# Matmul operands of a two-layer hybrid network moved to addresses that are multiples of 256 bytes

## The chip, the cores and the metric

The kernel runs on one core of one Trainium2 chip. The metric is device time in microseconds (us) of one execution; the median of three executions of the kernel before is 2283.09 us (2277.65 to 2285.34).

## The reference

Two layers over 512 tokens of 1024 channels. Each layer is a feed-forward block, a token mixer, and a second feed-forward block, each on an RMS norm of its input and added back; a last norm ends it. Layer 0 mixes with RWKV-7 and block attention, layer 1 with HGRN2. All of it is float32.

```python
def swiglu(h, w_gate, w_up, w_down):
    return (jax.nn.silu(h @ w_gate) * (h @ w_up)) @ w_down
...
    for l in range(DEPTH):
        x = x + 0.5 * swiglu(rmsnorm(x, norm_g[l, 0]), ffn1_wg[l], ffn1_wu[l], ffn1_wd[l])
        h = rmsnorm(x, norm_g[l, 1])
        if l % 2 == 0:
            p = h @ ev_w_in[e]
            y_a = rwkv7_mix(p[..., :RWKV_COLS], ...)
            y_b = moba_mix(p[..., RWKV_COLS:], slopes)
            y = jnp.concatenate([y_a, y_b], axis=-1) @ ev_w_out[e]
        else:
            y = hgrn2_mix(h @ od_w_in[o], lb_table[l], hg_norm_w[o]) @ od_w_out[o]
        x = x + y
        x = x + 0.5 * swiglu(rmsnorm(x, norm_g[l, 2]), ffn2_wg[l], ffn2_wu[l], ffn2_wd[l])
    return rmsnorm(x, final_g)
```

## The kernel before

**Tiling.** Channels lie on the 128 partitions, tokens along the free dimension. The 512 tokens are two streams of 256: stream 0 (A) and stream 1 (B). Both go through the same stages, one after the other or interleaved, so each stream has half of every kind of product.

**Three products for one.** A float32 product is made of three matmuls in the type float32r (`mm3`). The weights are split into a high plane `wh` and a low plane `wl`, the activations into `hh` and `hl` (input of a stage; `hh0`, `hl0` of stream 0 and `hh1`, `hl1` of stream 1) or `ah` and `al` (the inner activation of a feed-forward block). `mm3` multiplies high by high, low by high and high by low into one PSUM bank of the pool `pmm` (tile `m`). The weight block, 128 x 128, is the loaded operand; the activation plane, 128 x 256, is the one that streams through ("moving"). In `rows` (values of the mixers) it is the other way round: 512 columns of a weight plane stream, and a block of `hh` or `hl` is loaded.

**Jobs.** `run` goes through a list of jobs, one for each 128 x 1024 (or 128 x 768) piece of weights: a DMA from SyncE into `wr` (3 places), a copy of it into `wh` on ScalarE, the rest into `wl` on VectorE (3 places each), then the matmuls of the piece. Pieces are split two jobs ahead. A feed-forward block (`ffn`) has jobs `gate` and `up` (moving `hh`, `hl`) and `down` (moving `ah`, `al`). The mixers run as tasks whose steps `fill` puts between the matmuls by a rough model of the engines (`Clock`), which sees operations and tiles, not addresses. Their products go into tiles `b`, mostly as float32 matmuls, which the trace shows as two records each.

**Addresses.** Tiles come from pools (`K.__init__`: `cp` constants, `wp` weights, `hp` activations), and a pool lays its tags out in the order in which each is first asked for, in steps of 32 bytes. The allocation of the kernel before gives these places on every partition:

| planes | bytes from | multiple of 256 plus |
|---|---|---|
| `x0`, `x1` | 16512, 24704 | 128 |
| `wr`, `wh`, `wl` (all places) | 39232, 51520, 63808 | 64 |
| `hh0`, `hl0` | 76096, 84288 | 64 |
| `hh1`, `hl1` | 117632, 125824 | 128 |
| `ah`, `al` (all places) | 102144, 109312 | 0 |
| `acc`, `tmp` | 92480, 94528 | 64 |
| `tu`, `bc0` | 100096, 99072 | 0 |

The last column is called the residue below. Within a plane every moving operand begins at a multiple of 1024 bytes and every loaded block at a multiple of 512 bytes, so all operands of a plane have the plane's residue.

Of the kernel before, what the change touches and what calls it, by code (L numbers as in the profile page):

```python
# [22 lines left out]
# blocks of d_ff whose sums meet in PSUM, and the parts that a load takes  # L23
# [12 lines left out]
LEAD = -0.2  # L36

# [43 lines left out]
class Clock:  # L81
    """A rough model of when the engines get to their work; it only orders the program."""
# [8 lines left out]
    def tile(self, name, key, bufs):  # L91
        """a tile takes a free place, or the one that is done with first"""
        ring = self.slots.setdefault(key, [])
        rec = {"base": 0.0, "end": 0.0, "acc": []}
        if len(ring) < bufs:
            ring.append(rec)
        else:
            i = min(range(bufs), key=lambda x: ring[x]["end"])
            rec["base"] = rec["end"] = ring[i]["end"]
            ring[i] = rec  # L100
        self.recs[name] = rec
# [84 lines left out]
class Stream:  # L186
    """one half of the tokens"""


class K:  # L190
    def __init__(self, tc, ctx, a):
        self.tc, self.a = tc, a
        nc = self.nc = tc.nc
        self.clk = Clock()
        self.pe = Eng(nc.tensor, "pe", self.clk)
        self.v = Eng(nc.vector, "dve", self.clk)
        self.s = Eng(nc.scalar, "act", self.clk)
        self.g = Eng(nc.gpsimd, "pool", self.clk)
        self.q = Eng(nc.sync, "dma", self.clk)
        self.mm = self.pe.matmul  # L200
        self.n = 0
        self.tasks, self.named, self.marks = [], {}, {}
        self.pending, self.micro = [], []
        self.ticks, self.left = 0, 0.0
        self.cp = ctx.enter_context(tc.tile_pool(name="const", bufs=1))
        self.wp = ctx.enter_context(tc.tile_pool(name="wts", bufs=1))
        self.hp = ctx.enter_context(tc.tile_pool(name="act", bufs=1))
        self.ppm = ctx.enter_context(tc.tile_pool(name="pmm", bufs=3, space=PSUM))
        self.ppx = ctx.enter_context(tc.tile_pool(name="pmx", bufs=5, space=PSUM))
        self.st = []  # L210
        for i in range(2):
            st = Stream()
            st.i = i
            st.x = self.t(self.cp, [128, KT, N], F32, f"x{i}", 1)
            st.acc = None
            st.hready = 0.0
            self.st.append(st)
        self.par = self.t(self.cp, [128, NPAR], F32, "par", 1)
        self.cst = self.t(self.cp, [128, NCST], F32, "cst", 1)
        self.msk = self.t(self.cp, [128, NMSK], U8, "msk", 1)  # L220
        self.q.dma_start(self.st[0].x[:, 0:2], a["x"][0][:, 0:2])
        self.q.dma_start(self.par, a["par"])
        warm = self.t(self.cp, [128, 1], F32, "warm", 1)
        self.g.memset(warm, 0.0)
        self.s.activation(warm, warm, AF.Tanh)
        self.ident, self.id64, self.blk = self.c("ident"), self.c("id64"), self.c("blk")
        self.gmask, self.sel, self.ones = self.c("gmask"), self.c("sel"), self.c("ones")

    def loads(self):
        """what the first products do not wait for"""  # L230
        nc, a = self.nc, self.a
        self.q.dma_start(self.st[1].x, a["x"][1])
        n = CST["dist"][0]
        self.q.dma_start(self.cst[:, n:], a["cst"][:, n:])
# [8 lines left out]
    def t(self, pool, shape, dtype, tag, bufs):  # L243
        self.n += 1
        x = pool.tile(shape, dtype, tag=tag, name=f"{tag}_{self.n}", bufs=bufs)
        self.clk.tile(x.name, (id(pool), tag), bufs)
        return x

# [21 lines left out]
    # ---- order of the program: a list of jobs on the weights, and tasks that fill in  # L270
# [26 lines left out]
    def fill(self, until=0.0):  # L297
        """a step of a task that its engine need not wait for; more of them while PE waits anyway"""
        free = self.clk.free
        while True:  # L300
            now = max(free["pe"], until)
            full = max(free["dve"], free["act"]) > now + self.left + BACK
            for t in self.eligible():
                if t.ready <= max(now, free[t.eng]) + LEAD and (t.first or not full):
                    self.step(t)
                    break
            else:
                return
            if free["pe"] >= until:
                return  # L310
# [8 lines left out]
    def due(self, all):  # L319
        """the evacuations of the last jobs whose time has come"""  # L320
        now = [z for z in self.pending if all or not z[1]]
        self.pending = [(ev, hold - 1, name) for ev, hold, name in self.pending if hold and not all]
        for ev, _, name in now:
            if name:
                self.need(name)
            yield ev()
# [7 lines left out]
    def spread_out(self, done):  # L334
        """what goes along with a job, at its place in the job"""
        while self.micro and self.micro[0][0] <= done:
            self.micro.pop(0)[1]()
# [83 lines left out]
    # ---- pieces  # L421
# [4 lines left out]
    def mm3(self, out, w, x, first, last):  # L426
        """out += w^T x with w = (hi, lo) and x = (hi, lo)"""
        self.mm(out, w[0], x[0], start=first, stop=False)
        self.mm(out, w[0], x[1], start=False, stop=False)
        self.mm(out, w[1], x[0], start=False, stop=last)  # L430
        self.left -= out.free_size() / 800
        self.spread_out(1.0 - self.left / self.total)
        self.ticks += 1
        if self.ticks % TICK == 0:
            self.fill()
# [14 lines left out]
    # ---- rms norm of the columns of x^T: x * g goes into the products, and what they give is scaled  # L450
    def squares(self, st, i, last=False):
        """adds the squares of the pair i of row tiles; where PE has nothing else to do, it adds the rest"""
# [18 lines left out]
    def scaled(self, st, gi, i):  # L471
        """the pair i of row tiles of x^T * g, in two parts"""
# [10 lines left out]
    def inv_rms(self, st):  # L483
        """1 / rms, by token on the partitions"""
# [10 lines left out]
    def spread(self, st):  # L495
        """1 / rms on all partitions"""
# [25 lines left out]
    def norm(self, st, n):  # L522
        """starts the task of the norm n: (name, row of norm_g, whether it is done before the products)"""
# [29 lines left out]
    # ---- feed-forward  # L553
    def ffn(self, st, l, which, norm, then):
# [32 lines left out]
        def down(i, f0, f1, g0, g1):  # L587
            """the blocks f0 to f1 of the group g0 to g1"""
            def go(w):
# [4 lines left out]
                for d in range(2):  # L594
                    for j in range(m):
                        # the first product clears the marks of the bank, so that it opens both sums
# [31 lines left out]
        for f0, f1 in GRP:  # L628
            # one block past the group
# [12 lines left out]
    # ---- y^T (hi, lo) through the output projection, added to x^T  # L642
# [32 lines left out]
    def rows(self, st, srcs, evac):  # L675
        """h @ w for 512 columns, tokens on the partitions"""
# [24 lines left out]
    # ---- layer 0  # L701
# [22 lines left out]
    def proj0(self, st):  # L724
        """the jobs by part; the first of them waits for the scale"""
# [10 lines left out]
        def go(b, i):  # L736
            """the block b of columns, the first (i = 0) or the second of a pair that shares a bank"""
# [55 lines left out]
    # ---- MoBA: two blocks of 256 and one past block at most, so that a query sees all tokens up to it  # L793
    def moba(self, st):
        pool, v, s, mm, half = self.pool, self.v, self.s, self.mm, st.i
        for qi in range(2):
# [4 lines left out]
            for pr in range(4):  # L801
# [6 lines left out]
                for e, (sb, pe, sm) in enumerate(es):  # L808
                    # minus the scores, and minus their maximum
# [27 lines left out]
    # ---- RWKV-7: [channel of a pair of heads, pair, token]; chunks of 64 tokens  # L837
# [74 lines left out]
    def bcast(self, bc, rn):  # L912
        """[token, pair and head] -> [channel of a pair, pair, token]"""
# [70 lines left out]
    def rw_inv(self, env, c):  # L984
        """(I - A)^-1, the blocks on the diagonal doubled"""
# [56 lines left out]
    def rw_tail(self, st, q, env):  # L1042
        """norm per head, bonus, gate"""
# [7 lines left out]
        # r and k of these tokens end here  # L1051
# [28 lines left out]
    # ---- layer 1: HGRN2  # L1080
    def setup1(self, pool):
# [11 lines left out]
        # (1 - lb) / 2, its negative  # L1093
# [8 lines left out]
    def proj1(self, st, norm):  # L1102
# [9 lines left out]
        def go(b):  # L1112
            def f(w):
# [8 lines left out]
                def ev():  # L1122
# [10 lines left out]
                    if b < 16:  # L1133
                        th = self.t(self.hp, [128, 2, N], F32, "tmp", 2)
                        s.activation(th, o, AF.Tanh, scale=0.5)
                        for i in range(2):
                            c = j + i
                            # f = lb + (1 - lb) sigmoid, k = (1 - lb) (1 - sigmoid)
# [38 lines left out]
    def hg_levels(self, st, q, env):  # L1177
        """scores of 128 tokens: for every level, the second half of a block against the first; the
        products of the decays from the block's middle to either side stay in [0, 1]"""
# [109 lines left out]
# norms that end before the products that read them start  # L1289
# [3 lines left out]
def _cut(jobs, n):  # L1293
    """the first n jobs, and the rest; a negative n counts from the end"""
# [5 lines left out]
def _held(jobs, name, n):  # L1300
    """the first n jobs of a stage are evacuated together, after the task of the scale"""
# [47 lines left out]
def _tiles(w):  # L1349
    """[K, C] -> [C / 128, 128 (row in tile), K]: a block of 128 columns per entry"""  # L1350
# [5 lines left out]
def _down(w):  # L1356
    """[F, D] -> [D / 256, 128, 2 * F]: for a group of row tiles, 2 blocks of columns by the tiles"""
# [4 lines left out]
def _rows(w):  # L1362
    """[D, 512] -> [4, 128, 2 * 512]"""
    return np.ascontiguousarray(w.reshape(4, 2, 128, 512).transpose(0, 2, 1, 3).reshape(4, 128, 1024))
# [47 lines left out]
```

## Time and profile before

| | |
|---|---|
| median of three runs | 2283.09 us |
| span of the profiled execution | 2278.3 us |
| TensorE matmul busy | 2246.6 us (99%), 20476 records |
| VectorE, ScalarE busy | 1640.6 us (72%), 1061.7 us (47%) |
| granted TensorE clock, mean | 0.996 |

The profiled execution's own time is known by its span; it lies 4.8 us under the median and inside the spread of the three runs. "Busy" of TensorE counts matmuls from their start to their modelled end. They are pipelined and overlap, so what one costs is read from the distance between the starts of neighbours, not from its duration.

### The profile page before, as it was taken

What the parts mean: (1) busy time and instruction counts of PE and PEld (TensorE: products, weight loads), DVE (VectorE), ACT (ScalarE), POOL (GpSimd) and SP (SyncE); (2) the same over time, 40 slices, a digit from 0 to 9 for tenths busy, and PEclk for the clock granted to TensorE, in tenths of its full rate; (3) what the DMA queues carried; (4) which work ended last, traced back from release to release, by engine and by line L of the source; (5) the groups of instructions that cost most, each with busy time, mean ns of one, the idle gap of its engine ahead of it and who ended that gap; (6) DMA issues with size and microseconds to landing.
All of it is one profiled execution on the core that took longest, in us unless ns stands there. A gap on an engine that the chain in (4) does not pass through costs nothing.

```text
span 2278.3 us, 48851 instructions
## 1 busy us (share of the span) xinstructions
PE 2246.6 (99%) x20476; PEld 2176.9 (96%) x20476; DVE 1640.6 (72%) x2863; ACT 1061.7 (47%) x1716; POOL 3.7 (0%) x15
## 2 busy tenths in 40 slices
PE   8999999999999999999999999999999999999998
PEld 8999989899999888999998999999999999999998
DVE  6867758576677666776777786677777776767776
ACT  5545544345554434544454344454455334445444
POOL 0000000000000000000000000000000000000000
PEclk9999999999999999999999999999999999999999
DMA  6565524345554233456654345665665434556664
GB/s 224 180 198 175 172 87 137 96 133 178 190 168 157 74 103 98 147 163 182 181 189 157 130 139 151 190 179 178 192 183 172 151 118 154 160 185 195 191 191 136
DMA packets 107644, 363.64 MB, mean 160 GB/s; under 512 B 12064, under 2 KB 12192, under 8 KB 107296
## 3 DMA queue, kind: packets, MB, share of 16 engines
q1 hardware_dynamic: 107424, 360.53, 50.9%
q8 instruction: 160, 2.62, 0.5%
q14 instruction: 60, 0.49, 0.1%
HBM read 358.38 MB, written 2.10 MB: 158 GB/s over the span
## 4 chain that ended last, share of the span: by engine, by line
PE 93%; DVE 4%; ACT 2%; issue 1%; DMA 1%; SPq 0%; DVEq 0%; ACTq 0%
PE m L175 81%; PE b L175 12%; DVE wl L175 2%; ACT wh L175 1%; DMA wr<-in_f1gu 1%; DVE x L175 0%; DVE tmp L175 0%; DVE hl L175 0%; ACT hh L175 0%; DVE m L175 0%; DVE acc L175 0%; ACT tmp L175 0%; DVE rqz L175 0%; SPq L175 0%; ACT sh L175 0%
## 5 line engine op out<-in xcount | busy, mean ns | idle before, releaser
L175 PE MATMUL m<-hh,wh 128*128 128x256 f32 x3808 | 1095.9, 288 | 13.1 <-ACT wh L175 10.2
L175 PE MATMUL m<-hh,wl 128*128 128x256 f32 x3808 | 1074.2, 282 | 5.7 <-DVE wl L175 5.6
L175 PE MATMUL m<-hl,wh 128*128 128x256 f32 x3808 | 1073.7, 282 | 0.4
L175 DVE TENSOR_TENSOR wl<-wr,wh 128x1024 fp32r<-128x1024 f32 (+2 forms) x725 | 832.2, 1152 | 312.7 <-ACT wh L175 304.6
L175 ACT CAST wh<-wr 128x1024 fp32r<-128x1024 f32 (+2 forms) x725 | 712.7, 989 | 540.5 <-PE m L175 387.8
L175 PEld LDWEIGHTS m<-hh,wh 128*128 128x128 f32 x3808 | 724.6, 190 | 28.2 <-ACT wh L175 11.0
L175 PEld LDWEIGHTS m<-hh,wl 128*128 128x128 f32 x3808 | 724.3, 190 | 8.3 <-DVE wl L175 8.3
L175 PEld LDWEIGHTS m<-hl,wh 128*128 128x128 f32 x3808 | 724.6, 190 | 2.5 <-DVE hl L175 1.5
L175 PE MATMUL m<-ah,wh 128*128 128x256 f32 x1408 | 400.1, 284 | 0.0
L175 PE MATMUL m<-al,wh 128*128 128x256 f32 x1408 | 391.6, 278 | 0.0
L175 PE MATMUL m<-ah,wl 128*128 128x256 f32 x1408 | 391.4, 278 | 0.0
L175 PEld LDWEIGHTS m<-ah,wh 128*128 128x128 f32 x1408 | 264.5, 188 | 7.6 <-issue 5.1
L175 PEld LDWEIGHTS m<-ah,wl 128*128 128x128 f32 x1408 | 265.9, 189 | 0.0
L175 PEld LDWEIGHTS m<-al,wh 128*128 128x128 f32 x1408 | 264.9, 188 | 1.0 <-issue 1.0
L175 ACT CAST ah<-tu 128x256 fp32r<-128x256 f32 x176 | 71.5, 406 | 308.9 <-DVE tu L175 308.8
L175 DVE SCALAR_TENSOR_TENSOR tu<-tu,m 128x256 f32<-128x256 f32 x352 | 146.9, 417 | 6.5 <-ACT tu L175 0.5
L175 DVE TENSOR_TENSOR al<-tu,ah 128x256 fp32r<-128x256 f32 x176 | 74.9, 425 | 84.3 <-ACT ah L175 84.3
L175 DVE SCALAR_TENSOR_TENSOR x<-m,x 128x512 f32<-128x512 f32 x128 | 87.9, 687 | 20.3 <-PE m L175 20.0
L175 DVE TENSOR_TENSOR m<-m,bc 128x512 f32<-128x512 f32 x118 | 81.9, 696 | 21.5 <-PE m L175 16.8
L175 ACT ACTIVATE tu<-m 128x256 f32<-128x256 f32 x176 | 66.8, 380 | 21.0 <-DVE m L175 20.3
L175 PE MATMUL b<-Rq,Rk 128*128 128x128 f32 (+2 forms) x576 | 59.5, 252 | 0.0
L175 PEld LDWEIGHTS b<-Rq,Rk 128*128 128x128 f32 (+2 forms) x576 | 55.3, 167 | 3.8
(204 smaller groups left out, 1456.4 us busy)
## 6 DMA issues: line engine op xcount, KB each, us to landing
wr<-in_f2gu SPq DMA_DIRECT2D x176, 512.0 KB, 3.7
wr<-in_f1gu SPq DMA_DIRECT2D x175, 512.0 KB, 3.6
wr<-in_f1d SPq DMA_DIRECT2D x96, 384.0 KB, 3.3
wr<-in_f2d SPq DMA_DIRECT2D x96, 384.0 KB, 3.3
wr<-in_od_in SPq DMA_DIRECT2D x48, 512.0 KB, 3.4
wr<-in_ev_in SPq DMA_DIRECT2D x44, 512.0 KB, 3.3
wr<-in_f1d SPq DMA_DIRECT2D x16, 512.0 KB, 3.7
wr<-in_ev_out SPq DMA_DIRECT2D x16, 512.0 KB, 3.4
```

Of the source, the lines that this page charges most:

```text
L175: return f(*args, **kw)
```

## The change

No operation is added, removed or reordered. Only the order in which tags are first asked for changes, and with it the addresses. The constants `par`, `cst`, `msk`, `warm` are placed first, then a tile of 192 bytes that nothing uses, then `x0` and `x1`. A new helper `places` asks once for a tile of each plane, so that the planes lie first in their pools; the small tiles (`ms2`, `rqi`, `rqz`, `r0`, `r1`, `rqy`) come behind them.

```diff
+PAD = 192
...
+        self.par = self.t(self.cp, [128, NPAR], F32, "par", 1)
+        self.cst = self.t(self.cp, [128, NCST], F32, "cst", 1)
+        self.msk = self.t(self.cp, [128, NMSK], U8, "msk", 1)
+        warm = self.t(self.cp, [128, 1], F32, "warm", 1)
+        self.t(self.cp, [128, PAD], U8, "pad", 1)
         self.st = []
         for i in range(2):
...
-        self.par = self.t(self.cp, [128, NPAR], F32, "par", 1)
-        self.cst = self.t(self.cp, [128, NCST], F32, "cst", 1)
-        self.msk = self.t(self.cp, [128, NMSK], U8, "msk", 1)
+
+        self.places(self.wp, ("wr", KT * 128, F32, 1 + LOADS), ("wh", KT * 128, F32R, AHEAD + 1),
+                    ("wl", KT * 128, F32R, AHEAD + 1))
+        self.places(self.hp, *((f"{n}{i}", KT * N, F32R, 1) for i in range(2) for n in ("hh", "hl")),
+                    ("ah", N, F32R, 7), ("al", N, F32R, 7), ("acc", 2 * N, F32, 1), ("tmp", 2 * N, F32, 2),
+                    ("tu", N, F32, 2), ("bc0", N, F32, 1), ("bc1", N, F32, 1))
         self.q.dma_start(self.st[0].x[:, 0:2], a["x"][0][:, 0:2])
         self.q.dma_start(self.par, a["par"])
-        warm = self.t(self.cp, [128, 1], F32, "warm", 1)
         self.g.memset(warm, 0.0)
...
+    def places(self, pool, *tags):
+
+        for tag, n, dtype, bufs in tags:
+            self.n += 1
+            pool.tile([128, n], dtype, tag=tag, name=f"{tag}_{self.n}", bufs=bufs)
```

## Rows read from the trace of the kernel before

**Rows 1.** The page: busy time, and TensorE, VectorE and its clock in 40 slices.

```profile
PE 2246.6 (99%) x20476; PEld 2176.9 (96%) x20476; DVE 1640.6 (72%) x2863; ACT 1061.7 (47%) x1716; POOL 3.7 (0%) x15
...
DVE  6867758576677666776777786677777776767776
...
PEclk9999999999999999999999999999999999999999
```

**Rows 2.** The page: chain that ended last, as shares of the span.

```profile
PE 93%; DVE 4%; ACT 2%; issue 1%; DMA 1%; SPq 0%; DVEq 0%; ACTq 0%
PE m L175 81%; PE b L175 12%; DVE wl L175 2%; ACT wh L175 1%; DMA wr<-in_f1gu 1%; DVE x L175 0%; DVE tmp L175 0%; DVE hl L175 0%; ACT hh L175 0%; DVE m L175 0%; DVE acc L175 0%; ACT tmp L175 0%; DVE rqz L175 0%; SPq L175 0%; ACT sh L175 0%
```

**Rows 3.** Waits: engine, what for, total us, times, longest us.

```profile
ACT wh L175 <- PE m L175: 387.8, 263, 4.5
...
PE m L175 <- ACT wh L175: 10.2, 5, 5.8
...
PE m L175 <- DVE wl L175: 5.6, 9, 0.8
```

**Rows 4.** Groups of instructions: matmuls of the planes, count, busy us, mean ns.

```profile
L175 PE MATMUL m<-hh,wh 128*128 128x256 f32 x3808 | 1095.9, 288 | 13.1 <-ACT wh L175 10.2 <-ACT hh L175 2.7 <-ACT tmp L175 0.2
...
L175 PE MATMUL m<-al,wh 128*128 128x256 f32 x1408 | 391.6, 278 | 0.0
L175 PE MATMUL m<-ah,wl 128*128 128x256 f32 x1408 | 391.4, 278 | 0.0
...
L175 PE MATMUL m<-wh,hh 128*128 128x512 f32 x96 | 39.7, 414 | 0.7 <-ACT RV L175 0.7
```

**Rows 5.** Chain, unbroken gate/up stretches, stream 0, then 1: start, us, matmuls.

```profile
105.76 34.56 PE m L175 x288
...
1416.05 33.92 PE m L175 x288
```

**Rows 6.** Chain, unbroken down stretches, streams 0, 0, 1, 1: start, us, matmuls.

```profile
140.32 16.36 PE m L175 x144
...
1047.11 16.35 PE m L175 x144
...
1449.97 16.96 PE m L175 x144
...
1993.53 16.35 PE m L175 x144
```

**Rows 7.** Four of these stretches: us, busy (records) of PE, PEld, DVE, ACT, POOL; clock.

```profile
105.84:140.27 34.43, 34.43 (x289) 34.43 (x288) 26.87 (x40) 16.58 (x24) 0.00 (x0) 1.00 0.60 183
1416.12:1449.92 33.80, 33.80 (x289) 33.80 (x288) 22.33 (x32) 15.65 (x23) 0.00 (x0) 1.00 0.60 184
1047.18:1063.41 16.23, 16.23 (x145) 16.23 (x144) 11.38 (x15) 7.80 (x10) 0.00 (x0) 1.00 0.71 198
1450.05:1466.88 16.83, 16.83 (x145) 16.83 (x144) 10.22 (x13) 6.97 (x10) 0.00 (x0) 1.00 0.71 192
```

**Rows 8.** Groups within two stretches of rows 6, 1047.11 then 1449.97: count, mean ns.

```profile
L175 PE MATMUL m<-ah,wl 128*128 128x256 f32 x47 | 13.0, 276 | 0.0
...
L175 PE MATMUL m<-ah,wl 128*128 128x256 f32 x47 | 13.2, 281 | 0.0
```

**Rows 9.** Stretch at the lower granted clock, stream 0: clock, then first and tenth start.

```profile
1206.60:1209.80 3.20, 2.78 (x13) 2.78 (x14) 2.52 (x6) 1.56 (x2) 0.00 (x0) 0.50 0.47 164
...
1207.40 0.41 PE L175 MATMUL m<-hh,wh 128*128 128x256 f32 x1
...
1209.32 0.41 PE L175 MATMUL m<-hh,wh 128*128 128x256 f32 x1
```

**Rows 10.** 512-column matmuls, stream 0 then 1: first and eleventh start, us.

```profile
248.83 0.39 PE L175 MATMUL m<-wh,hh 128*128 128x512 f32 x1
...
251.10 0.39 PE L175 MATMUL m<-wl,hh 128*128 128x512 f32 x1
...
574.13 0.39 PE L175 MATMUL m<-wh,hl 128*128 128x512 f32 x1
...
576.46 0.39 PE L175 MATMUL m<-wh,hh 128*128 128x512 f32 x1
```

**Rows 11.** Timeline: eight records of mixer products, merged; `Rk` has residue 0, `kt` 64.

```profile
1237.71 1.05 PE L175 MATMUL b<-Rq,Rk 128*128 128x128 f32 x8
...
1305.35 1.05 PE L175 MATMUL b<-RV,kt 128*128 128x128 f32 x8
```

**Rows 12.** Groups: `AR`, `BK` at residue 192, `Plr`, `wa2` at 0; VectorE at 0, 64.

```profile
L175 PE MATMUL b<-AR,BK 64*128 64x128 f32 x128 | 13.7, 285 | 0.0
...
L175 PE MATMUL b<-Plr,wa 64*128 64x128 f32 x64 | 6.8, 285 | 0.0
...
L175 DVE TENSOR_TENSOR al<-tu,ah 128x256 fp32r<-128x256 f32 x176 | 74.9, 425 | 84.3 <-ACT ah L175 84.3
...
L175 DVE TENSOR_TENSOR acc<-acc 128x256 f32<-128x256 f32 x13 | 5.5, 426 | 0.4
```

More of the change, by code (lines that the diff above doesn't have):

```diff
@@ L186 @@
 class Stream:
+    pass
 class K:
```

## Prediction

> **What bounds the kernel now.** I read the page first. TensorE is busy 99% of the span, VectorE 72%, ScalarE 47%, and the clock slices are full [rows 1]. The chain of waits says the same from the other side: 81% of it are matmuls into `m`, the products with the weights, 12% matmuls into `b`, and VectorE and ScalarE together 6% [rows 2]. In the waits the split of the weights waits for the matmuls (ScalarE 387.8 us) and the matmuls hardly for it (10.2 and 5.6 us) [rows 3]. So the time is the number of matmuls into `m` times the distance between their starts, and the change can only matter by that distance. There are 3 x 3808 = 11424 of them with `hh`, `hl` moving, 5712 in each stream, and 3 x 1408 = 4224 with `ah`, `al` moving [rows 4].
>
> Then I looked for that distance where nothing interrupts it. Two gate/up stretches: 34.56 us for 288 matmuls in stream 0 is 120.0 ns each, 33.92 us for 288 in stream 1 is 117.8 ns [rows 5]. Same job, same shapes, same weights' places, both at the full granted clock [rows 7]; the planes of stream 0 have residue 64, those of stream 1 residue 128. Down stretches, whose planes have residue 0: 16.35 us for 144 is 113.5 ns, and 16.96 us for 144 is 117.8 ns [rows 6]. Of the twelve longest down stretches (143 steps each) six run at each of these paces; five of the six fast ones are in stream 0, and all six slow ones in stream 1 ([rows 6] holds the first and the last of the fast ones, and a slow one). 256 columns at 2.4 GHz would be 106.7 ns, so residues 64, 128 and 0 leave 13.3, 11.1 and 6.8 (or 11.1) ns on top. At the granted clock of 0.50 (1.2 GHz), with the planes of stream 0, nine steps take 1207.40 to 1209.32, that is 213.3 ns [rows 9]: 256 columns at 1.2 GHz, nothing on top. What depends on the place costs only at full rate.
>
> How often the down products run fast: their records last 276 ns in a fast stretch and 281 in a slow one [rows 8], 278 on the whole [rows 4], so 0.6 of them are fast and their mean pace is 0.6 x 113.5 + 0.4 x 117.8 = 115.2 ns.
>
> **The change, part by part.** By adding up tile sizes (488 bytes of `par` become 512, 4380 of `cst` 4384, 1408 of `msk`, 32 for `warm`, 192 of padding) `x0` moves from 16512 to 23040, and the planes `wr`, `wh`, `wl`, `hh0` ... `al` all land on residue 0. No instruction is removed, added or moved on any queue, and the order is made by a model that sees no addresses; so it costs nothing in instructions. The tile that `places` asks for is used by none, so nobody waits for it. Were it to keep one of three `wh` places, the one split still ahead has a job of 24 x 118 = 2.8 us as cover; I take 0.
>
> *Gate/up and other products with `hh`, `hl`.* The residue of the moving plane goes from 64 (stream 0) and 128 (stream 1) to 0. The nearest rows are the down stretches, residue 0 already: 113.5 to 117.8 ns. Within that I take 0.8 fast, 114.4 ns. It is above 0.6 because the slow down stretches lie in stream 1, right behind gate/up stretches of 117.8 ns, and stream 0 is fast; with all planes alike, the kind of stream 0 should win, but not everywhere.
> Stream 0: 5712 x (120.0 - 114.4) = 32.0 us.
> Stream 1: 5712 x (117.8 - 114.4) = 19.4 us.
>
> *Down products.* Moving residue stays 0. At 0.8 fast: 4224 x (115.2 - 114.4) = 3.4 us.
>
> *Loaded weight blocks*, residue 64 to 0. The trace has no 256-column matmul with another weight residue. Bounds: mixer products of 128 columns step the same with the loaded tile at 0 and at 64, 1.05 us for eight records both times [rows 11], so 0 is one end. The other ends are the rivals below. I take 0.
>
> *512-column matmuls* (288). Ten steps: 2.27 us with `hh0`/`hl0` loaded (residue 64), 2.33 us with `hh1`/`hl1` (128): 227 and 233 ns against 213.3 [rows 10]. Between 288 x 20 = 6 us gained and 2 us lost; I take 0.
>
> *Mixer tiles* come behind the planes and slide by 192 bytes, most from residue 0 to 192. The `b` products with tiles at 192 have the duration of those at 0, 285 ns both [rows 12]: 0. *VectorE and ScalarE*: 425 ns at residue 0 and 426 at 64 for the same size [rows 12]: 0. *DMA*: only `wr` and `x` move, and waits on them are 1% of the chain [rows 2]: 0.
>
> Sum on TensorE: 54.8 us. Not all of it reaches the end: 81% of the span is `m` on the chain [rows 2], whereas 15648 matmuls at about 118 ns plus 288 at 230 make 1912 us, 84%; and a faster PE reaches mixer results sooner than VectorE makes them. In the gate/up stretch VectorE is busy 26.87 of 34.43 us, 78%, and would be 82% [rows 7]: still not the bound there, though slices of 8 tenths exist elsewhere [rows 1]. I take 0.85 (between 0.5 and 1): 46.6 us. From the span that is 2231.7; I carry the 4.8 us by which it lies under the median: 2283.1 - 46.6 = 2236.5. What is late next is TensorE still, by its remaining 7.7 ns per matmul.
>
> **A rule that speaks against it.** The row: three residues, three paces [rows 5, 6]. The Trainium skill ("SBUF — State Buffer", Specifications) gives SBUF lines of 16 bytes and a penalty for each new line crossed. 64, 128 and 0 are all multiples of 16, so by that rule alone no plane is better placed than another and the sum would be 0. The trace does not agree in the paces, unless they come from something else; that is the second rival.
>
> **The rivals.**
> (1) *Slower: what counts is the moving address against the loaded one.* The two reads collide most when their residues are equal. Before, the difference is 0 in gate/up of stream 0, the slowest (120.0); 64 in stream 1 (117.8); 192 in down (113.5 or 117.8). After, it is 0 everywhere, and all run at 120.0: 5712 x 2.2 + 4224 x 4.8 = 12.6 + 20.3 = 33 us lost, 2316. It decides as soon as weights and planes share a residue, whichever it is. For it: weights never leave 64 in these rows, so the paces fit. Against it: with 512 columns, equal residues (both 64) are the faster case, 227 against 233 [rows 10]; and worst-to-best goes 64, 128, 0, the order of plain alignment, which a collision has no need to follow. The Trainium skill (same page, Who interferes with whom) gives TensorE two read ports that are independent, one for the moving and one for the loaded operand; by that this rival falls. No run here shows the ports.
> (2) *No change: the pace is a state, not the place.* Residue 0 already shows two paces for the same operands, each kept through a whole stretch [rows 6, 8]. If all stretches settle in the slow one, 5712 x 2.2 = 12.6 us come and 4224 x 2.6 = 11.0 go: 2281. Against it: 120.0 is not one of the two paces, and residue 64 keeps it.
> (3) *More: the loaded residue matters too.* The mixers' step is about 1.05 us less the last record's tail of 0.28, over seven steps, 110 ns [rows 11, 12]; at 111 everywhere 5712 x 9.0 + 5712 x 6.8 + 4224 x 4.2 = 108 us, times 0.85: 2191.
>
> **How the numbers follow.** Forecast 0.62; rival 1 0.18; rival 2 0.12; rival 3 0.08. The forecast's own range: all fast and all of it realised, 5712 x 6.5 + 5712 x 4.3 + 4224 x 1.7 = 69 us, 2214; share 0.6 and half realised, 5712 x 4.8 + 5712 x 2.6 = 42, half is 21, 2262. The range takes in rival 2 above and rival 3 below, and above it the half of rival 1's price: 2185 to 2300. About 0.3% (7 us) is what a measurement here can tell from none. Faster: forecast, rival 3 and a small part of rival 2, 0.71; same 0.11; slower 0.18.
>
> **What would show it.** Right: unbroken gate/up stretches of both streams with the same pace, 113.5 or 117.8, mostly the first; chain and waits as before. Wrong step by step: 120.0 in down stretches too (rival 1); 117.8 nearly everywhere (rival 2); under 113 (rival 3); the paces as forecast but more waits of TensorE on VectorE or ScalarE, which would make 0.85 too high.

## The result and the profile after

The changed kernel is slower: 2309.6 us (median of 4 runs, 2306.7 to 2311.2) against 2282.2 us before (4 runs), a ratio of 1.0115 with a 95% interval of 1.0097 to 1.0134. The forecast was 2236.5, with a range of 2185 to 2300; the first rival's 2316 is the nearest of the sums.

The page of the kernel after, in the parts that answer to [rows 1] and [rows 2], and two of its groups (count, busy us, mean ns) that answer to [rows 4]:

```profile
span 2308.1 us, 48851 instructions
...
PE 2278.4 (99%) x20476; PEld 2209.6 (96%) x20476; DVE 1642.8 (71%) x2863; ACT 1060.7 (46%) x1716; POOL 3.7 (0%) x15
...
PEclk9999999999999999999999999999999999999999
...
PE 91%; DVE 4%; ACT 2%; DMA 1%; issue 1%; SPq 0%; DVEq 0%; ACTq 0%
...
L176 PE MATMUL m<-al,wh 128*128 128x256 f32 x1408 | 398.2, 283 | 0.0
L176 PE MATMUL m<-ah,wl 128*128 128x256 f32 x1408 | 398.2, 283 | 0.0
```

The same instructions (20476 records on TensorE), the same clock, VectorE and ScalarE within 2.2 us of what they were. TensorE alone has grown, by 31.8 us busy, and the span by 29.8. A down product's record lasts 283 ns, where it was 278. The chain gives TensorE 91% where it gave 93%, so the loss is not to be read from its shares: the kernel with everything at residue 64 (below) has the same paces as this one, and `m` has 77.6% of its chain against 79.0% here.

The chain of the kernel after in four unbroken stretches: gate/up of stream 0, gate/up of stream 1, down of stream 0, down of stream 1 (start, us, matmuls). They answer to [rows 5] and [rows 6].

```profile
108.46 34.56 PE m L176 x288
...
1431.08 34.56 PE m L176 x288
...
1055.96 17.28 PE m L176 x144
...
1465.64 17.28 PE m L176 x144
```

34.56 / 288 and 17.28 / 144 are both 120.0 ns. The three paces of before have become one, and it is the slowest of them: stream 0 kept its 120.0, stream 1 lost 2.2 ns, and down lost 6.5 where it had been fast and 2.2 where it had been slow. No new wait explains the loss: ScalarE waits longer for TensorE to give weight places back, 430.2 us where [rows 3] has 387.8, and TensorE waits no longer than before for the split weights.

```profile
ACT wh L176 <- PE m L176: 430.2, 275, 4.5
...
PE m L176 <- ACT wh L176: 10.2, 4, 6.2
...
PE m L176 <- DVE wl L176: 4.9, 9, 0.8
```

### The profile page after: what moved, and what is told of

It is laid out like the page before. It is cut to its first block, busy times and chain, and to the rows that moved or that the text cites. A ratio compares the mean times of both kernels' runs of the same rounds, so it can differ in the third digit from the quotient of the medians.

```text
span 2308.1 us, 48851 instructions
## 1 busy us (share of the span) xinstructions
PE 2278.4 (99%) x20476; PEld 2209.6 (96%) x20476; DVE 1642.8 (71%) x2863; ACT 1060.7 (46%) x1716; POOL 3.7 (0%) x15
## 4 chain that ended last, share of the span: by engine, by line
PE 91%; DVE 4%; ACT 2%; DMA 1%; issue 1%; SPq 0%; DVEq 0%; ACTq 0%
PE m L176 79%; PE b L176 12%; DVE wl L176 2%; ACT wh L176 1%; DMA wr<-in_f1gu 1%; DVE tmp L176 0%; ACT sh L176 0%; DVE m L176 0%; DMA wr<-in_f2gu 0%; ACT hh L176 0%; DVE x L176 0%; DVE hl L176 0%; DMA wr<-in_ev_v 0%; DVE acc L176 0%; DMA wr<-in_ev_out 0%
## 5 line engine op out<-in xcount | busy, mean ns | idle before, releaser
L176 ACT CAST wh<-wr 128x1024 fp32r<-128x1024 f32 (+2 forms) x725 | 711.7, 988 | 573.8 <-PE m L176 430.2
L176 PEld LDWEIGHTS m<-hh,wh 128*128 128x128 f32 x3808 | 733.3, 193 | 26.7 <-ACT wh L176 11.0
L176 PEld LDWEIGHTS m<-hh,wl 128*128 128x128 f32 x3808 | 733.3, 193 | 7.1 <-DVE wl L176 7.0
L176 PEld LDWEIGHTS m<-hl,wh 128*128 128x128 f32 x3808 | 734.0, 193 | 2.1 <-DVE hl L176 1.1
L176 PE MATMUL m<-ah,wh 128*128 128x256 f32 x1408 | 406.7, 289 | 0.0
L176 PE MATMUL m<-al,wh 128*128 128x256 f32 x1408 | 398.2, 283 | 0.0
L176 PE MATMUL m<-ah,wl 128*128 128x256 f32 x1408 | 398.2, 283 | 0.0
L176 PEld LDWEIGHTS m<-ah,wh 128*128 128x128 f32 x1408 | 269.8, 192 | 7.6 <-issue 5.1
```

The lines of the kernel that those rows point to most:

```text
L176: return f(*args, **kw)
```

## The experiments

The planes lie as multiples of 256 bytes plus a residue, as in the table of addresses. Three theories. **D**: the pace depends on the difference of the moving and the loaded operand's residue. **L**: blocks loaded from residue 0 are slow. **M**: only the moving plane's alignment counts. All kernels run the same instructions in the same order as the two kernels compared; unused tiles shift the planes. Differences below are moving minus loaded, modulo 256. Paces are read from the chain in the two gate/up stretches and one down stretch of the same kind as above. The first kernel and the one with the weights alone moved ran four times, and their times are medians; the others ran once. The kernel before took 2280.0 us beside the first four kernels, 2282.5 beside the one with the weights alone, and 2282.1 (one run) beside the last four.

**Weights back to 64, planes at 0.** Against the changed kernel:

```diff
-        self.t(self.cp, [128, PAD], U8, "pad", 1)
...
-        self.places(self.hp, *((f"{n}{i}", KT * N, F32R, 1) for i in range(2) for n in ("hh", "hl")),
+        self.places(self.hp, ("gap0", 192, U8, 1), ("hh0", KT * N, F32R, 1), ("hl0", KT * N, F32R, 1),
+                    ("hh1", KT * N, F32R, 1), ("hl1", KT * N, F32R, 1), ...
```

> The changed kernel without the padding tile in front, and with 192 unused bytes ahead of hh0 instead: weight planes wr, wh, wl stay at residue 64 (as in the kernel before), all moving planes (hh, hl, ah, al of both streams) at residue 0. Difference of moving to loaded residue: 192 everywhere. Theory D (the difference counts): what down showed before, 113.5 or 117.8 ns per matmul, in gate/up too, and never 120.0; 2214 us if always 113.5, 2240 if six tenths are, 2281 if always 117.8. Theory M (the alignment of the moving plane alone counts, with something else in the changed kernel to blame for its loss): residue 0 moved in the changed kernel too, so 120.0 again and about 2310. Theory L (weights loaded from residue 0 are slow, wherever the moving plane lies): as theory D here, 113.5 to 117.8.

Measured: 2254.2 us, ratio to before 0.9887 (0.9871 to 0.9904), 55 us under the changed kernel. Four stretches of its chain, gate/up of stream 0, of stream 1, down of stream 1, gate/up of stream 1 again:

```profile
1046.83 32.64 PE m L175 x288
...
1393.80 33.92 PE m L175 x288
...
1616.01 16.96 PE m L175 x144
...
2142.50 32.64 PE m L175 x288
```

113.3, 117.8, 117.8 and 113.3 ns, none at 120.0. The moving planes are at residue 0 here as in the changed kernel, so M falls. Against the changed kernel, the weight planes (and `x0`, `x1`, which no matmul of the planes reads) lie 192 bytes lower; nothing else has moved. The kernel is the layout that the forecast had in mind: its down products had this difference before, and now gate/up has it too. It beats both kernels.

**Everything at 64.** The padding tile taken out of the changed kernel, nothing else.

```diff
-        self.t(self.cp, [128, PAD], U8, "pad", 1)
```

> The changed kernel without the padding tile: weight planes and all moving planes at residue 64, difference 0. Theory D: 120.0 ns in gate/up of both streams and in down, time as of the changed kernel, about 2310 us. Theory L (loaded residue 0 is slow): residue 64 is loaded, so down at least comes back to 113.5 to 117.8 and the time falls to 2290 or under. Theory M (moving alignment): 64 is the worst place, 120.0 or more, 2310 or above.

Measured: 2310.2 us. Gate/up of streams 0 and 1, and down:

```profile
106.49 34.56 PE m L175 x288
...
1430.50 34.56 PE m L175 x288
...
1055.50 17.28 PE m L175 x144
```

120.0 ns in all three. Residue 64 is loaded here, so L falls; with every operand on one residue, it makes no difference whether that is 0 or 64. What this kernel shares with the changed one is the difference 0.

**Other differences, weights at 0.** `places` gets unused tiles between the planes:

```diff
...
+        self.places(self.hp, ("gap0", 64, U8, 1), ("hh0", ...), ("hl0", ...), ("gap1", 64, U8, 1),
+                    ("hh1", ...), ("hl1", ...), ("gap2", 32, U8, 1), ("ah", ...), ("al", ...), ...
```

> Weight planes at residue 0 (as in the changed kernel); unused bytes between the planes put hh0/hl0 at 64, hh1/hl1 at 128, ah/al at 160: differences 64, 128, 160. Theory D: stream 0 gate/up 117.8 ns (difference 64, as stream 1 before), 128 and 160 not known, each its own pace, none 120.0; time between 2214 and 2290. Theory L: loaded residue 0 is slow, 120.0 in all three, 2310. Theory M: stream 0 (64) 120.0, stream 1 (128) 117.8, down (160) 120.0.

Measured: 2282.1 us. Differences 64, 128, 160, in this order:

```profile
104.82 33.92 PE m L176 x288
...
1413.50 34.18 PE m L176 x288
...
1043.48 16.90 PE m L176 x144
```

117.8, 118.7 and 117.4 ns. These are the paces of most stretches, not of all: each of these differences shows a second pace in some (last section). The difference 64 paces at 117.8 with weights at 0 as it did with weights at 64 and planes at 128 [rows 5].

**Other differences, weights at 64.** No padding tile; gaps of 32, 64 and 128 bytes ahead of `hh0`, `hh1`, `ah`.

```diff
-        self.t(self.cp, [128, PAD], U8, "pad", 1)
...
+        self.places(self.hp, ("gap0", 32, U8, 1), ("hh0", ...), ("hl0", ...), ("gap1", 64, U8, 1),
+                    ("hh1", ...), ("hl1", ...), ("gap2", 128, U8, 1), ("ah", ...), ("al", ...), ...
```

> Weight planes at residue 64; hh0/hl0 at 96, hh1/hl1 at 160, ah/al at 32: differences 32, 96, 224, none a multiple of 64. Theory D: each its own pace by the difference; were collisions by lines of 64 bytes alone, 32 would pace as 0 or as 64 (120.0 or 117.8), 96 as 64 or 128, 224 as 192 or 0. Theory M (alignment of the moving plane): 96, 160 and 32 are all multiples of 32 only, so all three alike and at least as slow as 120.0, 2310 us or more. Theory L: 113.5 to 117.8 in all.

Measured: 2289.1 us. Differences 32, 96, 224:

```profile
105.54 33.60 PE m L175 x288
...
1417.46 34.56 PE m L175 x288
...
1046.66 17.03 PE m L175 x144
```

116.7, 120.0 and 118.3 ns. Three planes aligned alike (to 32 bytes only) have three paces, and one of them is better than two of the three "rounder" ones before. The guess by lines of 64 bytes (32 as 0 or 64, 224 as 192 or 0) missed too: 116.7 and 118.3 are none of these paces.

**The change's one part alone: the weights.** The kernel before, with the weight planes moved to 0 and everything behind them held at its residue.

```diff
         warm = self.t(self.cp, [128, 1], F32, "warm", 1)
+        self.t(self.cp, [128, 192], U8, "pad", 1)
+        self.t(self.hp, [128, 64], U8, "gap", 1)
```

> The kernel before with one part of the change alone: 192 unused bytes ahead of the weight planes and 64 behind them, so that wr, wh, wl lie at residue 0 and every moving plane keeps the residue it had (hh0/hl0 64, hh1/hl1 128, ah/al 0). Theory D (the difference counts): differences 64, 128, 0 instead of 0, 64, 192; by the paces of the other kernels stream 0 gains 5712 x (119.9 - 117.6) = 13 us, stream 1 loses 5712 x (118.7 - 117.7) = 6 us, down loses 4224 x (119.9 - 115.1) = 20 us: 13 us slower than before, about 2295 us, with down alone at 120.0. Theory L (blocks loaded from residue 0 are slow): 120.0 in all three, about 2310. Theory M (the moving residue alone counts): nothing changes, 2282.

Measured: 2295.3 us, ratio 1.0055 (1.0035 to 1.0075), 12.7 us slower where 13 were expected. Stream 0 (difference 64), stream 1 (128), down (0):

```profile
106.79 33.93 PE m L175 x288
...
1423.84 34.18 PE m L175 x288
...
1050.59 17.26 PE m L175 x144
```

117.8, 118.7, 119.9 ns. No moving plane changed its residue, and all three paces changed, one down and two up. This is D with its size, although the prices were taken from kernels in which these three differences had already been measured with weights at 0. `wr` moves with `wh` and `wl` in every kernel here; TensorE does not read it, but its part was not tried by itself.

**Which two operands meet.** The two weight planes at different residues (`wh` 64, `wl` 128), `hh` and `ah` at 0, `hl` and `al` at 64:

```diff
-        self.t(self.cp, [128, PAD], U8, "pad", 1)
...
-        self.places(self.wp, ("wr", ...), ("wh", ...), ("wl", ...))
+        self.places(self.wp, ("wr", ...), ("wh", ...), ("gapw", 64, U8, 1), ("wl", ...))
+        self.places(self.hp, ("gap0", 128, U8, 1), ("hh0", ...), ("hh1", ...), ("ah", ...),
+                    ("gap1", 64, U8, 1), ("hl0", ...), ("hl1", ...), ("al", ...), ...
```

> Which two operands meet: wh at residue 64, wl at 128, hh and ah at 0, hl and al at 64. In mm3 the matmul hh x wh streams while the wh of the next matmul is loaded, hl x wh while wl is loaded, hh x wl while the next wh is loaded. Theory C (a moving operand meets the block loaded for the NEXT matmul): differences hh-wh 192, hl-wl 192, hh-wh 192, so 113.5 or 117.8 ns as in w64_a0, 2235 to 2260 us. Theory O (it meets the block of its OWN matmul): hh-wh 192, hl-wh 0, hh-wl 128, so a mean of about (115.5 + 120.0 + 118.7) / 3 = 118.1 ns and about 2295 us.

Measured: 2294.6 us; the mean step inside unbroken stretches is 118.5 ns in all three kinds. The reverse, with `gap0` at 192, so that `hh`, `ah` are at 64 and `hl`, `al` at 128:

> The reverse: wh at 64, wl at 128, hh and ah at 64, hl and al at 128. Theory C: differences of what is under way at the same time are hh-wh 0, hl-wl 0, hh-wh 0: 120.0 ns everywhere, about 2310 us, although moving and loaded residues of two of three matmuls differ. Theory O: hh-wh 0, hl-wh 64, hh-wl 192, a mean of about (120.0 + 117.7 + 115.5) / 3 = 117.7 ns, about 2274 us.

Measured: 2279.9 us, mean step 117.8 ns in all three. C said 115.5 and 120.0, O said 118.1 and 117.7. C, in the plain form that the expectation gives it, is out: with a difference of 0 between what streams and what is recorded as being loaded beside it, the pace is not 120.0. O hits both means but not the steps behind them. After `hh` x `wh`, `hl` x `wh` and `hh` x `wl` (for down, the same with `ah` and `al`) the next matmul starts 119.4, 118.1 and 118.1 ns later in the first kernel, where O asks for 115.5, 120.0 and 118.7, and 118.3, 117.2 and 117.9 ns later in the reverse, where O asks for 120.0, 117.7 and 115.5. However the three are shifted against the steps, at least one step is off by 1.9 ns or more, so the steps do not bear out what the means suggest.

**Two layouts meant to lose the slow pace of the difference 192.** Weights at 64, `hh` and `ah` at 0, and the low planes elsewhere (first 96, 160, 32; then 128, 192, 224, for `hl0`, `hl1`, `al`):

```diff
-        self.t(self.cp, [128, PAD], U8, "pad", 1)
...
+        self.places(self.hp, ("gap0", 32, U8, 1), ("hl0", ...), ("gap1", 64, U8, 1), ("hl1", ...),
+                    ("gap2", 96, U8, 1), ("hh0", ...), ("hh1", ...), ("ah", ...), ("gap3", 32, U8, 1), ("al", ...), ...
```

> Weights at 64, hh0, hh1, ah at 0 (difference 192); hl0 at 96 (32), hl1 at 160 (96), al at 32 (224). A search for a place without the slow pace of 117.8. Theory C: only the one of three matmuls that streams hl or al changes against w64_a0; its mean was 115.5; from the paces at differences 32, 96, 224 (116.9, 119.9, 118.3) two thirds of 115.5 and one third of these: 116.0 in stream 0, 117.0 in stream 1, 116.4 in down, 2254 to 2280 us, unless the mixture breaks the slow state, then 113.5 and 2220.

> Weights at 64, hh0, hh1, ah at 0 (192); hl0 at 128 (64), hl1 at 192 (128), al at 224 (160). As mix1: two thirds of 115.5 and one third of 117.6, 118.7, 117.6: 116.2, 116.6, 116.2 ns, 2260 to 2275 us, unless the mixture breaks the slow state, then 113.5 and 2220.

Measured: 2285.5 us both times, 5 us over the top of the first range and 10 us over that of the second. Mean steps 118.6, 117.8, 118.9 ns (stream 0, stream 1, down) in the first and 117.8, 118.8, 117.8 in the second, 0.8 to 2.6 ns over the weighted means. So where residues are mixed the pace is not the mean of the pure paces. The means of all four kernels with mixed residues lie between 117.8 and 118.9 ns, which leaves little that a theory of means could show. Which two operands meet stays open.

## Why the prediction was wrong

**What bounds the kernel: right.** TensorE still sets the time, by the distance between its matmuls, and the span followed it: the steps of uninterrupted plane matmuls add up to 1762.7 us before and 1793.7 after, 31.0 more, for 29.8 us of span. TensorE is idle for 31.7 us of the span before and for 29.7 after.

**The step that failed** is "Loaded weight blocks, residue 64 to 0 ... I take 0". The bound for it came from mixer products of 128 columns, where the loaded tile's place made no difference [rows 11]. Those step at 110 ns with half the columns streaming, and the row does not say where their moving tiles lie; it does not answer for a stream of 256 columns. What the weights' place is worth was seen twice: the kernel that differs from the changed one by it (weights at 64, planes at 0) runs 55 us faster, and the kernel before with the weights alone moved from 64 to 0 runs 12.7 us slower. So this term, put at 0, turned a gain of 26 us (planes at 0, weights left at 64) into a loss of 27. With it went the reading of the three residues as three qualities of the moving plane. They were differences to the weights: 0, 64 and 192.

**Rival 1** named the mechanism, its point ("as soon as weights and planes share a residue, whichever it is": both 0 and both 64 gave 120.0) and came near with its price: 33 us, measured 27. The paces were as it said, 120.0 ns in stream 1 and in down; the unbroken steps give 31.0 of the 33 us, the span 29.8 and the medians 27.4.

**Rivals 2 and 3** fell: 117.8 was not the pace everywhere, and no kernel here paces under 113.3. But rival 2 was right that one place can have two paces; see the last section.

**The argument used against rival 1** was weak in two places. The order 64, 128, 0 as an order of alignment was an accident of where the planes lay: in the fourth kernel the planes at 96 and 160, aligned alike, pace at 116.7 and 120.0. And the 512-column rows [rows 10] had the equal residues faster, 227 against 233 ns. That holds (228 at equal residues in the changed kernel, 233 with differences of 192 and 128 in the third kernel), but there the weight plane streams and the activation is loaded, and the order of 256 columns is not that of 512.

**The rules of the Trainium skill.** The prediction took from the Trainium skill ("SBUF — State Buffer", Specifications) lines of 16 bytes and a penalty for each new line crossed. By that alone all the places tried here, multiples of 32, are alike; the runs do not agree, with 113.3 to 120.0 ns among them. It also took from the Trainium skill (same page, Who interferes with whom) that TensorE's two read ports are independent, which spoke against rival 1. The runs do not bear the conclusion out: moving the loaded operand alone took down products from a mean of 115.1 to 119.9 ns, so in effect the two operands are not independent of each other. Whether ports, banks or something behind them are shared, no run shows.

**The size of the gain** that was forecast can be checked too, since the first experiment is the layout that it describes. It brought 26 us where 46.6 were forecast. The share of fast stretches was the term that was off: 0.8 was taken, and the mean step there is 115.5, 115.8 and 115.4 ns (stream 0, stream 1, down), half fast and half slow, close to the 0.6 that the down products showed before. The factor 0.85 was about right: 5712 x (119.9 - 115.5) + 5712 x (117.7 - 115.8) - 4224 x 0.3 = 34.7 us on TensorE, of which 26 (medians) to 30 (spans) arrived, a factor of 0.75 to 0.87.

The reason given for 0.8 was a misreading of the kernel before. It has sixteen unbroken down stretches of 143 steps, not twelve: ten fast, seven in stream 0 and three in stream 1, and six slow, all in stream 1. The last one of [rows 6], at 1993.53, belongs to stream 0. The fast ones of stream 1 lie behind gate/up stretches at 117.8 ns as the slow ones do, so these did not decide. Gate/up of stream 1 and the down stretch behind it (start, us, matmuls), 117.8 and 113.5 ns:

```profile
2120.16 33.57 PE m L175 x285
...
2153.97 16.11 PE m L175 x142
```

**The other terms taken as 0** held: the 4234 steps between mixer products add up to 243.3 us before and 243.2 after, VectorE and ScalarE are busy as long as before to within 2.2 us, DMA stays at 1% of the chain. Two groups of [rows 12] after the change:

```profile
L176 PE MATMUL b<-AR,BK 64*128 64x128 f32 x128 | 13.7, 285 | 0.0
...
L176 DVE TENSOR_TENSOR acc<-acc 128x256 f32<-128x256 f32 x13 | 5.5, 425 | 0.4
```

`AR`, `BK` went from 192 to 128 and `acc` from 64 to 0, with the same durations (425 ns for 426). `AR` and `BK` moved together, so the difference between them stayed what it was; these rows do not show what another difference would do to a mixer product.

## What to carry to other kernels

In a kernel whose float32r matmuls follow one another without a gap, compare the distance between their starts by where the planes lie, both operands of each pair; here a table of pace by difference told more than rounding addresses up. Laying all operands on the same multiple put every pair on a difference whose pace is the slowest in the table below, and the same planes with the weights 192 bytes lower took 2.4% less time. And a bound for a cost is only as good as the row's likeness to the case: a row with other shapes, which tells the place of one operand and not of the other, bounds nothing where two places meet.

## What the runs showed of the hardware

**Pace by difference.** A matmul of 256 float32r columns on a 128 x 128 block, at the full granted clock, in unbroken stretches where all planes of a kind share a residue. 256 columns at 2.4 GHz are 106.7 ns. Where a second pace follows an "also", the first is that of most stretches.

| moving minus loaded, modulo 256 | ns per matmul | seen with the loaded block at |
|---|---|---|
| 0 | 120.0 | 64, 0 |
| 32 | 116.7; also 117.8 | 64 |
| 64 | 117.8; also 113.3 | 64, 0 |
| 96 | 120.0 | 64 |
| 128 | 118.7; also 120.0 | 0 |
| 160 | 117.4; also 118.7 | 0 |
| 192 | 113.3 or 117.8 | 64 |
| 224 | 118.3 | 64 |

The second paces, one stretch each (start, us, matmuls): difference 32 in the fourth kernel, 64 and 160 in the third, 128 in the one with the weights alone moved.

```profile
1215.99 14.13 PE m L175 x120
...
909.93 13.38 PE m L176 x118
...
1636.64 16.97 PE m L176 x143
...
1334.83 5.40 PE m L175 x45
```

That the difference decides, whatever the residues, was tried for 0 and 64 alone, the two seen with the loaded block at 64 and at 0. A period of 128 is out (0 and 128 differ, so do 64 and 192). The period of 256 rests on 192: modulo 512 it is 448 in the down products of the kernel before and 192 in the first experiment, with the same two paces.

At the lower granted clock the kernel before ran at 213.3 ns with a difference of 0 [rows 9], the bare columns; other differences were not looked at there.

**One difference, two paces.** With the difference 192 an unbroken stretch is fast or slow as a whole: in the first experiment's kernel, none of 121 stretches of 18 steps or more has halves whose paces differ by over 2 ns. One fast stretch there lasts for 1196 matmuls (113.5 ns) and one slow one for 1560 (117.8 ns), both through gate/up and down alike (chain: start, us, matmuls):

```profile
1009.12 135.76 PE m L175 x1196
...
1500.35 183.74 PE m L175 x1560
```

The timeline shows the start of the slow one, then that of the fast one (start, us):

```profile
1500.11 0.36 PE L175 MATMUL m<-hh,wh 128*128 128x256 f32 x1
1500.31 0.28 PE L175 MATMUL m<-hl,wh 128*128 128x256 f32 x1
...
1009.05 0.38 PE L175 MATMUL m<-hh,wh 128*128 128x256 f32 x1
1009.27 0.28 PE L175 MATMUL m<-hl,wh 128*128 128x256 f32 x1
```

The first step after the pause is 0.20 us in the slow one and 0.22 us in the fast one. Over that whole execution there are 160 stretches of nine steps or more. Of 61 that began with a step of 219 to 224 ns 52 were fast, of 79 that began with 199 to 207 ns 51 were slow, and of the 20 others 17 were fast. So the longer first step goes with the faster stretch, but does not settle it. What sets that step was not tried, and no layout was found that has the pace of 113.3 alone.
